# Down projection of a hybrid encoder layer: weight differences in place on VectorE, four fixed operand buffers, another order at the hand-overs

## The chip, the core and the metric

One core of a Trainium2 chip runs the whole program in one launch. The metric is the device time of one execution in microseconds, as the median of several runs. Engines: TensorE multiplies matrices, VectorE and GpSimd do elementwise work, ScalarE does elementwise functions, SyncE's queue (SP) starts the transfers of this part. A matrix product reads operands from SBUF and sums into PSUM.

## What is computed

One layer of an encoder over 512 tokens of width 1024: a mixer of three head groups, a cross-attention into 256 memory tokens, and a gated MLP of inner width 2816 with a causal convolution of width 3. The change lies in the MLP's down projection, the last step.

```python
def conv_ffn(xn, w_up, conv_w, conv_b, w_down):
    h = xn @ w_up
    a, b = jnp.split(h, 2, axis=-1)
    ...
    return (jax.nn.gelu(c, approximate=False) * b) @ w_down

h = h + conv_ffn(rmsnorm(h, ffn_norm_g[l]), ffn_w_up[l], ...)
```

Here `c` is the convolution of `a` along the tokens plus a bias.

## The kernel before

All matrix products are made in three parts: every operand x is split into a high part (ScalarE copies it to the reduced type that TensorE takes) and a low part (VectorE subtracts the high part from x), and high·high, low·high and high·low are summed in PSUM. `split` (lines 325 and 326) makes the two parts.

The up projection goes through 11 groups, `up_group` (line 1353). Each has four PSUM tiles `pa` and `pb` (two of each, 128 features by 512 tokens). Behind the matmuls of a group comes its gating: VectorE reads PSUM with the token scale (lines 1365 and 1372), ScalarE and VectorE make the convolution, ScalarE the GELU, VectorE the product (lines 1375 and 1378). The gated result of group g is two feature blocks of 128, "even" and "odd", over 512 tokens.

The down projection (512 x 2816 times 2816 x 1024) is made with seven block products in place of eight, a Strassen-Winograd scheme. The tokens are halved, the 1024 columns are halved, and each pair of feature blocks (k = 0 to 10) gives the inner halves. So block k has token operands a11, a12, a21, a22 and weights W11, W12, W21, W22 of 128 x 512 each. `operands` (line 1274) makes the token sums. The weight differences are t1 = W12 - W11, t2 = W22 - t1, t3 = W22 - W12, t4 = W21 - t2. The products have numbers: 1 is a11 W11, 6 a sum times t2, 7 a sum times t3, 5 a sum times t1, 2 is a12 W21, 4 is a22 t4, 3 is a sum times W22. A product of one block is six matmuls: two tiles of 128 tokens, three parts each.

The order is a list written out by the code. The first pass, `seq1` (line 1296), takes products 1, 6, 7, 5 for blocks 0 and 1 together, then block by block, then the last two blocks together. The second pass, `seq2` (line 1298), takes products 2, 4, 3, for blocks 0 to 2 together, then singly, then the last two together. Each product sums over all blocks in its own pair of PSUM banks `X[p]`; product 2 goes on summing onto the banks of product 1, product 4 onto those of 7, product 3 onto those of 5, so the second pass continues on sums that VectorE has combined at the end of the first (lines 1427 to 1441: `u2` is products 1 + 6, and so on). The finished quarters of the output are added to the residual `h2T` and stored by `store` (line 1406).

The weights are prepared ahead of their product: `wahead(n)` (line 1341) traces the loads (`wload`, line 1310, on SP's queue) and the preparation (`wprep`, line 1318) three products ahead and at high priority. `wprep` makes t1 and t2 on VectorE (lines 1323, 1324), t3 and t4 on GpSimd (lines 1327, 1330), splits the raw token operands for the second pass (line 1333, 768 columns wide) and splits the weights (line 1338). Raw W11 and W21 lie in a ring of three buffers (`wraw`), the other weights and t2 in a ring of 18 (`r`), of which 16 hold the up projection's token operands until it ends; t1, t3 and t4 lie in a ring of five (`t`). High and low weight parts have rings of five each (`whi`, `wlo`). A scheduler sets the order of the instructions on each engine, by the order of tracing, the priorities and its own timing model; each engine then works its instructions off in that order.

Of the kernel before, what the change touches and what calls it, by code (L numbers as in the profile page):

```python
# [12 lines left out]
AF = mybir.ActivationFunctionType  # L13
# [193 lines left out]
def trunk_body(ctx: ExitStack, tc: tile.TileContext, A):  # L207
# [1061 lines left out]

    op1, op2, raw2 = {}, {}, {}

    def operands(g, even):

# [12 lines left out]
        else:  # L1288
# [6 lines left out]

    seq1 = [(p, k) for ks in ((0, 1), *((k,) for k in range(2, NG - 2)), (NG - 2, NG - 1))
            for p in (1, 6, 7, 5) for k in ks]
    seq2 = [(p, k) for ks in ((0, 1, 2), *((k,) for k in range(3, NG - 2)), (NG - 2, NG - 1))
            for p in (2, 4, 3) for k in ks]
    seq = seq1 + seq2  # L1300
    wd = A["wd"]
    BLK = {"11": 0, "12": 1, "22": 2, "21": 3}
# [15 lines left out]
    def wprep(n):  # L1318
        p, k = seq[n]
        R = lambda b: wr[n >= len(seq1), k, b]  # L1320
        if p == 6:
            wt[1, k], wt[2, k] = ts(), rs()
            V.tensor_tensor(wt[1, k], R("12"), R("11"), ALU.subtract)
            V.tensor_tensor(wt[2, k], R("22"), wt[1, k], ALU.subtract)
        elif p == 7:
            wt[3, k] = ts()
            G.tensor_tensor(wt[3, k], R("22"), R("12"), ALU.subtract)  # L1327
        elif p == 4:
            wt[4, k] = ts()
            G.tensor_tensor(wt[4, k], R("21"), wt[2, k], ALU.subtract)  # L1330
        elif p == 2:
            hi, lo = ma(), ma()
            split(raw2[k], hi[:, 0:3], lo[:, 0:3])
            op2[k] = [(hi[:, i], lo[:, i]) for i in range(3)]
        src = {1: lambda: R("11"), 6: lambda: wt[2, k], 7: lambda: wt[3, k], 5: lambda: wt[1, k],
               2: lambda: R("21"), 4: lambda: wt[4, k], 3: lambda: R("22")}[p]()
        hi, lo = wring("whi", WCFG[2], F32R), wring("wlo", WCFG[3], F32R)
        split(src, hi, lo)
        wx[n] = (hi, lo)
# [13 lines left out]
    def up_group(g):  # L1353
        pa, pb = [ps("a0"), ps("a1")], [ps("b"), ps("b")]
        funit(pa, h2n, range(0, 4), True, False)
        funit(pb, h2n, range(0, 4), True, False)
        funit(pa, h2n, range(4, 8), False, True)
        if g == NG - 1:
            wahead(2)
        funit(pb, h2n, range(4, 8), False, True)  # L1360
        cw = lambda tap, i: pv[:, PC["ffn_conv_w"] + 22 * tap + i:PC["ffn_conv_w"] + 22 * tap + i + 1]
        for c in range(2):
            i = 2 * g + c
            a = ts()
            V.tensor_tensor(a, pa[c], rb2, ALU.mult)
            ca = ts()
            ACT.activation(ca, a, AF.Identity, scale=cw(2, i), bias=pcol("ffn_conv_b", i))
            V.scalar_tensor_tensor(ca[:, 1:S], a[:, 0:S - 1], cw(1, i), ca[:, 1:S], ALU.mult, ALU.add)
            V.scalar_tensor_tensor(ca[:, 2:S], a[:, 0:S - 2], cw(0, i), ca[:, 2:S], ALU.mult, ALU.add)
            ACT.activation(ca, ca, AF.Gelu)  # L1370
            b = ts()
            V.tensor_tensor(b, pb[c], rb2, ALU.mult)
            if c == 0:
                even = b
                V.tensor_tensor(b, b, ca, ALU.mult)
            else:
                raw2[g] = t2("raw2", NG, (P, 3, 256))
                V.tensor_tensor(raw2[g][:, 0:2].rearrange("p a t -> p (a t)"), b, ca, ALU.mult)  # L1378
        operands(g, even)
        if g < 8:  # L1380
            t, l = g % 4, g // 4
            pt = pd("hT")
            for k in range(4):
                PE.transpose(pt[:, k * P:(k + 1) * P], h2[4 * l + k][:, t * P:(t + 1) * P], ident)
            h2T[t, l] = dsl()
            ACT.activation(h2T[t, l], pt, AF.Copy)

    for g in range(NG):
        up_group(g)

    X = {1: [ps("pr") for _ in range(2)], 6: [ps("pd") for _ in range(2)],
         7: [ps("a0"), ps("a1")], 5: [ps("b") for _ in range(2)]}
# [19 lines left out]
    u2 = p5 = None  # L1412
    for n, (p, k) in enumerate(seq):
        wahead(n + 3)
        last = k == NG - 1
        if p == 3 and k >= NG - 2:
            if last:
                for tt in range(2):
                    for m in (n - 1, n):
                        product(m, tt)  # L1420
                    store(0, 1, tt, X[3][tt], h2T[tt, 1])
            continue
        for tt in range(2):
            product(n, tt)
        if not last:
            continue
        if p == 6:
# [4 lines left out]
        elif p == 7:  # L1432
            for tt in range(2):
                V.tensor_tensor(X[7][tt], X[7][tt], u2[:, tt], ALU.add)
        elif p == 5:
            p5 = ma((P, 2, 512), F32)
            for tt in range(2):
                V.tensor_tensor(p5[:, tt], X[5][tt], h2T[2 + tt, 1], ALU.add)
                V.tensor_tensor(X[5][tt], X[5][tt], u2[:, tt], ALU.add)
            for tt in range(2):  # L1440
                store(1, 1, tt, X[7][tt], p5[:, tt])
        elif p == 2:
            for tt in range(2):
                store(0, 0, tt, X[2][tt], h2T[tt, 0])
        elif p == 4:
            for tt in range(2):
                store(1, 0, tt, X[4][tt], h2T[2 + tt, 0])


# [15 lines left out]
```

## Time and profile before

| what | value |
|---|---|
| median of 3 runs | 831.75 us |
| lowest and highest run | 829.24 and 833.24 us |
| the profiled execution's own time | 833.35 us |
| its span in the profile | 831.6 us |
| mean granted TensorE clock of the span | 0.979 |
| TensorE, matmul busy | 799.7 us (96%) |
| VectorE busy | 560.6 us (67%) |
| ScalarE busy | 413.8 us (50%) |
| GpSimd busy | 195.8 us (24%) |

The profile covers one execution. Busy times of an engine say nothing of what waits for what; matmuls overlap in their records, so a busy TensorE is read with the distance from start to start. The granted clock is the share of 2.4 GHz that TensorE was given. Times below are microseconds from the start of the span; the down projection's first matmul begins at 709.78.

### The profile page before, as it was taken

What the parts mean: (1) busy time and instruction counts of PE and PEld (TensorE: products, weight loads), DVE (VectorE), ACT (ScalarE), POOL (GpSimd) and SP (SyncE); (2) the same over time, 40 slices, a digit from 0 to 9 for tenths busy, and PEclk for the clock granted to TensorE, in tenths of its full rate; (3) what the DMA queues carried; (4) which work ended last, traced back from release to release, by engine and by line L of the source; (5) the groups of instructions that cost most, each with busy time, mean ns of one, the idle gap of its engine ahead of it and who ended that gap; (6) DMA issues with size and microseconds to landing.
All of it is one profiled execution on the core that took longest, in us unless ns stands there. A gap on an engine that the chain in (4) does not pass through costs nothing.

```text
span 831.6 us, 11606 instructions
## 1 busy us (share of the span) xinstructions
PE 799.7 (96%) x4130; PEld 659.2 (79%) x4130; DVE 560.6 (67%) x987; ACT 413.8 (50%) x766; POOL 195.8 (24%) x196
## 2 busy tenths in 40 slices
PE   8998997999999998999999999999999999899798
PEld 5775786789897886888888888888888888688586
DVE  6758389356796855745656666666666667997974
ACT  7343453556788854545554444434344334445552
POOL 6556274285741100000100000000000000332440
PEclk9999998999999999999999999999999999999899
DMA  6422022123121334221112322222222223364221
GB/s 206 153 77 75 27 83 96 39 72 108 53 102 38 115 119 135 91 100 51 51 56 97 115 89 101 90 89 101 89 101 90 101 99 105 110 194 142 98 77 76
DMA packets 43625, 79.22 MB, mean 95 GB/s; under 512 B 4784, under 2 KB 5936, under 8 KB 43568
## 3 DMA queue, kind: packets, MB, share of 16 engines
q1 hardware_dynamic: 41328, 75.35, 26.8%
q10 hardware_dynamic: 2240, 3.15, 1.2%
q8 instruction: 32, 0.52, 0.3%
q14 instruction: 25, 0.20, 0.1%
HBM read 76.38 MB, written 2.10 MB: 94 GB/s over the span
## 4 chain that ended last, share of the span: by engine, by line
PE 79%; DVE 6%; ACT 4%; issue 1%; DVEq 0%; ACTq 0%
PE ps L344 19%; PE ps L345 18%; PE ps L346 18%; PE ps L1403 10%; DVE b L658 1%; DVE b L657 1%; PE T L587 1%; DVE wlod L326 1%; DVE ma L326 1%; PE S L344 1%; PE colsum L407 1%; PE tr L535 1%; ACT whid L325 1%; ACT wh L184 1%; PE S L345 1%
## 5 line engine op out<-in xcount | busy, mean ns | idle before, releaser
L184 ACT ACTIVATE wh<-wr 128x512 fp32r<-128x512 f32 x212 | 133.0, 629 | 191.1 <-PE ps L345 130.2
L187 DVE TENSOR_TENSOR wl<-wr,wh 128x512 fp32r<-128x512 f32 x176 | 124.2, 706 | 81.4 <-ACT wh L184 77.1
L344 PE MATMUL ps<-r,wh 128*128 128x512 f32 x416 | 162.2, 393 | 3.1 <-ACT r L325 3.0
L346 PE MATMUL ps<-r,wl 128*128 128x512 f32 x416 | 162.4, 393 | 0.7 <-DVE wl L187 0.7
L345 PE MATMUL ps<-r,wh 128*128 128x512 f32 x416 | 163.0, 392 | 0.0
L344 PEld LDWEIGHTS ps<-r,wh 128*128 128x128 f32 x416 | 78.2, 188 | 20.0 <-ACT r L325 3.7
L1403 PE MATMUL ps<-whid,ma 128*128 128x512 f32 x276 | 89.1, 402 | 4.9 <-ACT whid L325 4.0
L346 PEld LDWEIGHTS ps<-r,wl 128*128 128x128 f32 x416 | 78.7, 189 | 17.8 <-DVE wl L187 1.1
L345 PEld LDWEIGHTS ps<-r,wh 128*128 128x128 f32 x416 | 78.6, 189 | 16.3 <-issue 0.2
L1327 POOL TENSOR_TENSOR t<-r,r 128x512 f32<-128x512 f32 x11 | 18.1, 1646 | 266.5 <-DVE raw L1378 237.8
L344 PE MATMUL ps<-wh,xh 128*128 128x256 f32 (+1 forms) x224 | 72.1, 345 | 8.2 <-DVE d L329 4.7
L345 PE MATMUL ps<-wl,xh 128*128 128x256 f32 (+1 forms) x224 | 77.8, 347 | 0.0
L1403 PEld LDWEIGHTS ps<-whid,ma 128*128 128x128 f32 x276 | 53.6, 195 | 17.1 <-ACT whid L325 4.8
L187 POOL TENSOR_TENSOR wl<-wr,wh 128x512 fp32r<-128x512 f32 x36 | 52.9, 1478 | 31.1 <-ACT wh L184 30.9
L1403 PE MATMUL ps<-wlod,ma 128*128 128x512 f32 x138 | 55.2, 400 | 2.7 <-DVE wlod L326 2.7
L344 PEld LDWEIGHTS ps<-wh,xh 128*128 128x128 f32 x224 | 42.5, 192 | 13.9 <-DVE d L329 4.9
L345 PEld LDWEIGHTS ps<-wl,xh 128*128 128x128 f32 x224 | 43.2, 193 | 5.1 <-issue 0.9
L345 PE MATMUL ps<-xl,wh 128*128 128x512 f32 x112 | 44.7, 402 | 0.0
L346 PE MATMUL ps<-wh,xl 128*128 128x512 f32 x96 | 39.1, 408 | 0.0
L345 PE MATMUL ps<-d,wh 128*128 128x512 f32 x96 | 37.7, 392 | 0.0
L346 PE MATMUL ps<-d,wl 128*128 128x512 f32 x96 | 37.5, 390 | 0.0
L346 PE MATMUL ps<-wh,xh 128*128 128x256 f32 x128 | 37.1, 289 | 0.0
(349 smaller groups left out, 1606.4 us busy)
## 6 DMA issues: line engine op xcount, KB each, us to landing
wr<-in_wp_dram SPq DMA_DIRECT2D x212, 256.0 KB, 2.6
r<-in_wd_dram SPq DMA_DIRECT2D x33, 256.0 KB, 3.5
wrawd<-in_wd_dram SPq DMA_DIRECT2D x22, 256.0 KB, 2.7
r<-in_xt_dram SPq DMA_DIRECT2D x8, 256.0 KB, 5.1
t<-in_xt_dram ACTq DMA_DIRECT2D x8, 256.0 KB, 2.8
out_dram<-t SPq DMA_DIRECT2D x8, 256.0 KB, 2.1
kv<-in_memt_dram ACTq DMA_DIRECT2D x4, 256.0 KB, 4.2
pm<-in_pmat_dram SPq DMA_DIRECT2D x1, 512.0 KB, 4.2
```

What stands on the lines that cost most here:

```text
L184: nc.scalar.activation(hi, raw, AF.Copy)
L187: (nc.vector if el == "V" else nc.gpsimd).tensor_tensor(lo, raw, hi.bitcast(F32), ALU.subtract)
L325: ins = ACT.activation(dhi, src, AF.Copy)
L326: V.tensor_tensor(dlo, src, dhi.bitcast(F32), ALU.subtract)
L344: mm(out, lh, rh, start=start, stop=False)
L345: mm(out, lh, rl, start=False, stop=False)
L346: mm(out, ll, rh, start=False, stop=stop)
L407: mm(pt[:, 2 * i:2 * i + 2], tot[:, i * P:(i + 1) * P], ones[:, 0:2], start=True, stop=True)
L535: PE.transpose(pv4[0:n, c, p, :], src(p, 2 * q + c), ident)
L587: mm(pts[hh].rearrange("p (c h t) -> p c h t", c=2, h=2)[:, c, p], KB[p][o:o + 64, cg, :], RA[p][o:o + 64, cg, :], start=True, stop=True)
L1327: G.tensor_tensor(wt[3, k], R("22"), R("12"), ALU.subtract)
L1403: mm(X[p][tt], l, r, start=not onto and k == 0 and j == 0, stop=k == NG - 1 and j == 2, skip_group_check=onto)
```

## The change

1. In `wprep`, all four differences are made on VectorE and written over their inputs: t1 over W12, t2 over W22, t4 over t2; t3 has a buffer of its own in the ring `r`. GpSimd does nothing more in this stage.
2. The raw token operands of the second pass are split into four fixed pairs of buffers (`ob`), block k into pair k mod 4.
3. `seq2` takes products 2, 3, 4 in place of 2, 4, 3, and the first four blocks together. The last quarter to be stored is now that of product 4.
4. In the last up group the four PSUM tiles are read first (`read`), and the rest of the gating (`rest`) is traced only after six products of the down projection; one more product is prepared ahead of it.
5. At the end of the first pass `p5` is copied by ScalarE, then product 7's sums are added to it; the residual is added and the quarter stored only after product 4 of block 3 is traced.

```diff
@@ seq2
-    seq2 = [(p, k) for ks in ((0, 1, 2), *((k,) for k in range(3, NG - 2)), (NG - 2, NG - 1))
-            for p in (2, 4, 3) for k in ks]
+    seq2 = [(p, k) for ks in ((0, 1, 2, 3), *((k,) for k in range(4, NG - 2)), (NG - 2, NG - 1))
+            for p in (2, 3, 4) for k in ks]
@@ wprep
         if p == 6:
-            wt[1, k], wt[2, k] = ts(), rs()
-            V.tensor_tensor(wt[1, k], R("12"), R("11"), ALU.subtract)
-            V.tensor_tensor(wt[2, k], R("22"), wt[1, k], ALU.subtract)
-        elif p == 7:
-            wt[3, k] = ts()
-            G.tensor_tensor(wt[3, k], R("22"), R("12"), ALU.subtract)
+            wt[3, k], wt[1, k], wt[2, k] = rs(), R("12"), R("22")
+            V.tensor_tensor(wt[3, k], wt[2, k], wt[1, k], ALU.subtract)
+            V.tensor_tensor(wt[1, k], wt[1, k], R("11"), ALU.subtract)
+            V.tensor_tensor(wt[2, k], wt[2, k], wt[1, k], ALU.subtract)
         elif p == 4:
-            wt[4, k] = ts()
-            G.tensor_tensor(wt[4, k], R("21"), wt[2, k], ALU.subtract)
+            V.tensor_tensor(wt[2, k], R("21"), wt[2, k], ALU.subtract)
         elif p == 2:
-            hi, lo = ma(), ma()
+            if k < 4:
+                ob.append((ma(), ma()))
+            hi, lo = ob[k % 4]
             split(raw2[k], hi[:, 0:3], lo[:, 0:3])
@@ up_group
         if g == NG - 1:
-            wahead(2)
+            wahead(3)
...
+        if g == NG - 1:
+            for src, dst in ((pa, av), (pb, bv)):
+                for c in range(2):
+                    read(src, dst, c)
+            return rest
+        rest()
@@ the loop over the products
         wahead(n + 3)
+        if n == 6:
+            rest()
...
+        if p == 4 and k == 3:
+            for tt in range(2):
+                store(1, 1, tt, p5[:, tt], h2T[2 + tt, 1])
...
         elif p == 5:
             p5 = ma((P, 2, 512), F32)
             for tt in range(2):
-                V.tensor_tensor(p5[:, tt], X[5][tt], h2T[2 + tt, 1], ALU.add)
+                ACT.activation(p5[:, tt], X[5][tt], AF.Copy)
                 V.tensor_tensor(X[5][tt], X[5][tt], u2[:, tt], ALU.add)
             for tt in range(2):
-                store(1, 1, tt, X[7][tt], p5[:, tt])
+                V.tensor_tensor(p5[:, tt], X[7][tt], p5[:, tt], ALU.add)
```

**VectorE between the projections, before.** The piece from the last PSUM read of the last up group (`ps_940`) to the low weight part of product 6 of block 1 (`wlod_979`).

```order
L1372 TENSOR_TENSOR t_960_6916<-ps_940_6762,rb_161_892 128x512
L1369 SCALAR_TENSOR_TENSOR t_959_6911<-t_958_6909,pv_78,t_959_6911 128x510
L1323 TENSOR_TENSOR t_976_6945<-r_945_6855,wrawd_942_6849 128x512
L1378 TENSOR_TENSOR raw2_961_6918<-t_960_6916,t_959_6911 128x512
L1324 TENSOR_TENSOR r_977_6946<-r_946_6857,t_976_6945 128x512
L1279 TENSOR_TENSOR sm_962_6920<-t_957_6906,raw2_961_6918 128x256
L1281 TENSOR_TENSOR sm_962_6920<-sm_962_6920,t_957_6906 128x256
L326 TENSOR_TENSOR wlod_979_6950<-r_977_6946,whid_978_6949 128x512
```

The low part stands behind the last PSUM read and most of the last group's gating.

**VectorE between the projections, now.** The low part of product 6 of block 1 is `wlod_957`, its source `r_946`; the last PSUM read is again that of `ps_940`.

```order
L326 TENSOR_TENSOR wlod_953_6872<-r_944_6853,whid_952_6871 128x512
L1365 TENSOR_TENSOR t_960_6913<-ps_939_6761,rb_161_892 128x512
L1323 TENSOR_TENSOR r_985_6991<-r_971_6933,r_970_6931 128x512
L1323 TENSOR_TENSOR r_1005_7069<-r_982_6979,r_981_6977 128x512
L1324 TENSOR_TENSOR r_970_6931<-r_970_6931,wrawd_954_6875 128x512
L326 TENSOR_TENSOR wlod_957_6882<-r_946_6857,whid_956_6881 128x512
L1324 TENSOR_TENSOR r_981_6977<-r_981_6977,wrawd_978_6965 128x512
L1365 TENSOR_TENSOR t_961_6915<-ps_940_6762,rb_161_892 128x512
L1325 TENSOR_TENSOR r_971_6933<-r_971_6933,r_970_6931 128x512
L326 TENSOR_TENSOR wlod_973_6936<-r_951_6867,whid_972_6935 128x512
```

The low part now stands ahead of the last PSUM read, and differences of blocks 2 and 3 stand around it; the gating follows, spread between later rows.

**VectorE between the passes, before.** From the combination of product 7's sums (`ps_971`, `ps_972`) to the third operand split of the second pass's later blocks (`ma_1179`); the low part of product 4 of block 0 comes four rows behind the piece.

```order
L1434 TENSOR_TENSOR ps_971_6939<-ps_971_6939,ma_1116_7465 128x512
L326 TENSOR_TENSOR wlod_1127_7503<-wrawd_1106_7427,whid_1126_7502 128x512
L1434 TENSOR_TENSOR ps_972_6940<-ps_972_6940,ma_1116_7465 128x512
L326 TENSOR_TENSOR wlod_1132_7519<-wrawd_1110_7441,whid_1131_7518 128x512
L1438 TENSOR_TENSOR ma_1133_7528<-ps_973_6941,d_890_6206 128x512
L1439 TENSOR_TENSOR ps_973_6941<-ps_973_6941,ma_1116_7465 128x512
L1438 TENSOR_TENSOR ma_1133_7528<-ps_974_6942,d_906_6393 128x512
L1439 TENSOR_TENSOR ps_974_6942<-ps_974_6942,ma_1116_7465 128x512
L326 TENSOR_TENSOR ma_1157_7616<-raw2_837_5627,ma_1156_7615 128x768
L326 TENSOR_TENSOR ma_1168_7656<-raw2_853_5814,ma_1167_7655 128x768
L1409 TENSOR_TENSOR t_1134_7533<-ps_971_6939,ma_1133_7528 128x512
L326 TENSOR_TENSOR ma_1179_7696<-raw2_869_6001,ma_1178_7695 128x768
```

Splits for blocks 3 and later stand between the additions and ahead of product 4's weights.

**VectorE between the passes, now.** The last 12 of the 24 rows from the operand split of block 0 (`ma_1101`) to the low part of product 3 of block 1 (`wlod_1122`); `ps_968`, `ps_969` are product 5's sums, `ps_966`, `ps_967` product 7's.

```order
L1327 TENSOR_TENSOR r_982_6979<-wrawd_1092_7433,r_982_6979 128x512
L1459 TENSOR_TENSOR ps_968_6923<-ps_968_6923,ma_1095_7445 128x512
L1461 TENSOR_TENSOR ma_1114_7512<-ps_966_6921,ma_1114_7512 128x512
L326 TENSOR_TENSOR ma_1116_7520<-raw2_837_5627,ma_1115_7519 128x768
L326 TENSOR_TENSOR wlod_1118_7524<-wrawd_1092_7433,whid_1117_7523 128x512
L1327 TENSOR_TENSOR r_1002_7057<-wrawd_1125_7563,r_1002_7057 128x512
L326 TENSOR_TENSOR wlod_1120_7534<-r_1096_7450,whid_1119_7533 128x512
L1459 TENSOR_TENSOR ps_969_6924<-ps_969_6924,ma_1095_7445 128x512
L1461 TENSOR_TENSOR ma_1114_7512<-ps_967_6922,ma_1114_7512 128x512
L1424 TENSOR_TENSOR t_1147_7662<-ma_1114_7512,d_890_6206 128x512
L1327 TENSOR_TENSOR r_1014_7107<-wrawd_1133_7599,r_1014_7107 128x512
L326 TENSOR_TENSOR wlod_1122_7544<-r_1099_7462,whid_1121_7543 128x512
```

Only the split of block 3 is left in this piece; splits of later blocks have moved behind it, and differences of product 4 (line 1327) stand in it.

**VectorE in the second pass, now.** The last three differences of product 4 (`L1327`, of blocks 8, 9 and 10), each with its block 21 as `wrawd`; the buffer of `wrawd_1167` is free after `wlod_1158`, that of `wrawd_1170` after `wlod_1166`.

```order
L326 TENSOR_TENSOR wlod_1158_7708<-wrawd_1141_7637,whid_1157_7707 128x512
L1327 TENSOR_TENSOR r_1050_7257<-wrawd_1159_7717,r_1050_7257 128x512
L326 TENSOR_TENSOR ma_1101_7465<-raw2_917_6562,ma_1100_7464 128x768
L326 TENSOR_TENSOR wlod_1161_7720<-r_1144_7649,whid_1160_7719 128x512
L326 TENSOR_TENSOR wlod_1164_7733<-r_1026_7157,whid_1163_7732 128x512
L1327 TENSOR_TENSOR r_1065_7319<-wrawd_1167_7754,r_1065_7319 128x512
L326 TENSOR_TENSOR wlod_1166_7745<-wrawd_1151_7680,whid_1165_7744 128x512
L326 TENSOR_TENSOR ma_1106_7483<-raw2_931_6742,ma_1105_7482 128x768
L326 TENSOR_TENSOR wlod_1169_7757<-r_1154_7692,whid_1168_7756 128x512
L326 TENSOR_TENSOR wlod_1172_7770<-r_1038_7207,whid_1171_7769 128x512
L1327 TENSOR_TENSOR r_1070_7337<-wrawd_1170_7766,r_1070_7337 128x512
```

Before, these differences stood on GpSimd, whose queue held nothing else here; now low parts of other products stand behind them.

## Rows read from the trace of the kernel before

**Rows 1.** Windows of 10 us: length, busy us (instructions) by engine, clock, DMA share, GB/s.
```profile
core 0: us, PE busy (x) PEld busy (x) DVE busy (x) ACT busy (x) POOL busy (x), PEclk, DMA share, GB/s
...
710.00:720.00 10.00, 7.36 (x26) 5.41 (x25) 9.90 (x16) 4.90 (x9) 3.70 (x3) 0.87 0.53 179
720.00:730.00 10.00, 10.00 (x43) 8.17 (x43) 10.00 (x12) 3.87 (x7) 4.31 (x3) 0.96 0.37 110
...
770.00:780.00 10.00, 8.71 (x39) 6.88 (x37) 10.00 (x14) 6.69 (x11) 2.41 (x2) 1.00 0.26 81
780.00:790.00 10.00, 6.43 (x16) 4.47 (x17) 9.53 (x14) 3.21 (x7) 5.83 (x1) 0.66 0.29 105
```

**Rows 2.** Waits of TensorE from 700 to the end: us in total, times, longest.
```profile
PE ps L1403 <- ACT whid L325: 4.0, 2, 3.3
PE ps L1403 <- DVE wlod L326: 2.7, 2, 2.0
PE ps L1403 <- DVE t L1409: 0.9, 1, 0.9
```

**Rows 3.** Groups of instructions by form, 660 to the end: the down projection's matmuls.
```profile
L1403 PE MATMUL ps<-whid,ma 128*128 128x512 f32 x276 | 89.1, 402 | 4.9 <-ACT whid L325 4.0 <-DVE t L1409 0.9
L1403 PE MATMUL ps<-wlod,ma 128*128 128x512 f32 x138 | 55.2, 400 | 2.7 <-DVE wlod L326 2.7
...
L1403 PE MATMUL ps<-whid,d 128*128 128x512 f32 x32 | 10.0, 389 | 0.0
...
L1403 PE MATMUL ps<-wlod,d 128*128 128x512 f32 x16 | 6.2, 389 | 0.0
```

**Rows 4.** Timeline of TensorE: start, length, instruction, count, idle time before it.
```profile
709.78 0.39 PE L1403 MATMUL ps<-whid,ma 128*128 128x512 f32 x1
...
714.70 0.73 PE L1403 MATMUL ps<-whid,ma 128*128 128x512 f32 x2 [0.67 <-ACT whid L325]
717.40 0.76 PE L1403 MATMUL ps<-wlod,ma 128*128 128x512 f32 x1 [1.97 <-DVE wlod L326]
...
758.60 0.39 PE L1403 MATMUL ps<-wlod,ma 128*128 128x512 f32 x1
...
759.96 0.39 PE L1403 MATMUL ps<-wlod,ma 128*128 128x512 f32 x1
...
778.32 0.39 PE L1403 MATMUL ps<-whid,ma 128*128 128x512 f32 x1
781.99 0.48 PE L1403 MATMUL ps<-whid,ma 128*128 128x512 f32 x1 [3.29 <-ACT whid L325]
783.37 1.65 PE L1403 MATMUL ps<-whid,ma 128*128 128x512 f32 x3 [0.89 <-DVE t L1409]
...
827.12 0.39 PE L1403 MATMUL ps<-whid,ma 128*128 128x512 f32 x1
```

**Rows 5.** The chain that ended last: start, length, its longest piece of the second pass.
```profile
785.70 41.36 PE ps L1403 x174
```

**Rows 6.** Timelines of GpSimd (first row) and VectorE (the others).
```profile
719.30 1.66 POOL L1327 TENSOR_TENSOR t<-r,r 128x512 f32<-128x512 f32 x1 [2.84 <-DVE wlod L326]
...
719.75 1.76 DVE L326 TENSOR_TENSOR wlod<-t,whid 128x512 fp32r<-128x512 f32 x1
721.44 0.68 DVE L1324 TENSOR_TENSOR r<-r,t 128x512 f32<-128x512 f32 x1
722.04 1.28 DVE L326 TENSOR_TENSOR wlod<-t,whid 128x512 fp32r<-128x512 f32 x2
```

**Rows 7.** Timelines of ScalarE and VectorE: cast and low part of an operand, 768 wide.
```profile
766.54 0.84 ACT L325 ACTIVATE ma<-raw 128x768 fp32r<-128x768 f32 x1
...
781.77 0.94 DVE L326 TENSOR_TENSOR ma<-raw,ma 128x768 fp32r<-128x768 f32 x1
```

**Rows 8.** GpSimd's wait for block 21; landings of W11 and W21; loads of 694 to 735.
```profile
POOL t L1330 <- DMA wrawd<-in_wd_dram: 10.8, 4, 4.8
...
DMA to landing us min/median/max: 2.4/2.7/5.2
...
r<-in_wd_dram SPq DMA_DIRECT2D x14, 256.0 KB, 4.1
```

More of the change, by code (lines that the diff above doesn't have):

```diff
@@ L1262, in ma @@
         return t2("ma", 18, shape, dt)
-    op1, op2, raw2 = {}, {}, {}
+    op1, op2, raw2, ob = {}, {}, {}, []
     def operands(g, even):
@@ L1335, in wprep @@
         src = {1: lambda: R("11"), 6: lambda: wt[2, k], 7: lambda: wt[3, k], 5: lambda: wt[1, k],
-               2: lambda: R("21"), 4: lambda: wt[4, k], 3: lambda: R("22")}[p]()
+               2: lambda: R("21"), 4: lambda: wt[2, k], 3: lambda: R("22")}[p]()
         hi, lo = wring("whi", WCFG[2], F32R), wring("wlo", WCFG[3], F32R)
@@ L1358, in up_group, with read, gated @@
         if g == NG - 1:
-            wahead(2)
+            wahead(3)
         funit(pb, h2n, range(4, 8), False, True)
         cw = lambda tap, i: pv[:, PC["ffn_conv_w"] + 22 * tap + i:PC["ffn_conv_w"] + 22 * tap + i + 1]
-        for c in range(2):
+        av, bv = {}, {}
+        def read(src, dst, c):
+            dst[c] = ts()
+            V.tensor_tensor(dst[c], src[c], rb2, ALU.mult)
+        def gated(c):
             i = 2 * g + c
-            a = ts()
-            V.tensor_tensor(a, pa[c], rb2, ALU.mult)
-            ca = ts()
+            a, ca = av[c], ts()
             ACT.activation(ca, a, AF.Identity, scale=cw(2, i), bias=pcol("ffn_conv_b", i))
@@ L1370, in up_group, with rest @@
             ACT.activation(ca, ca, AF.Gelu)
-            b = ts()
-            V.tensor_tensor(b, pb[c], rb2, ALU.mult)
+            if c not in bv:
+                read(pb, bv, c)
             if c == 0:
-                even = b
-                V.tensor_tensor(b, b, ca, ALU.mult)
+                V.tensor_tensor(bv[c], bv[c], ca, ALU.mult)
             else:
                 raw2[g] = t2("raw2", NG, (P, 3, 256))
-                V.tensor_tensor(raw2[g][:, 0:2].rearrange("p a t -> p (a t)"), b, ca, ALU.mult)
-        operands(g, even)
+                V.tensor_tensor(raw2[g][:, 0:2].rearrange("p a t -> p (a t)"), bv[c], ca, ALU.mult)
+        def rest():
+            for c in range(2):
+                if c not in av:
+                    read(pa, av, c)
+                gated(c)
+            operands(g, bv[0])
+        if g == NG - 1:
+            for src, dst in ((pa, av), (pb, bv)):
+                for c in range(2):
+                    read(src, dst, c)
+            return rest
+        rest()
         if g < 8:
@@ L1388, in trunk_body @@
     for g in range(NG):
-        up_group(g)
+        rest = up_group(g)
     X = {1: [ps("pr") for _ in range(2)], 6: [ps("pd") for _ in range(2)],
@@ L1414, in trunk_body @@
         wahead(n + 3)
+        if n == 6:
+            rest()
         last = k == NG - 1
-        if p == 3 and k >= NG - 2:
+        if p == 4 and k >= NG - 2:
             if last:
@@ L1420, in trunk_body @@
                         product(m, tt)
-                    store(0, 1, tt, X[3][tt], h2T[tt, 1])
+                    store(1, 0, tt, X[4][tt], h2T[2 + tt, 0])
             continue
@@ L1444, in trunk_body @@
                 store(0, 0, tt, X[2][tt], h2T[tt, 0])
-        elif p == 4:
+        elif p == 3:
             for tt in range(2):
-                store(1, 0, tt, X[4][tt], h2T[2 + tt, 0])
+                store(0, 1, tt, X[3][tt], h2T[tt, 1])
 def kernel(**inputs):
```

## Prediction

> **What bounds the kernel now.** I read the windows of ten microseconds first. Everywhere but in two places of the down projection TensorE is busy all the time; in 710 to 720 it has 7.36 of 10 us, in 770 to 780 8.71, in 780 to 790 6.43, and the granted clock means 0.87 in the first and 0.66 in the last (1.00 is 2.4 GHz, 0.50 is 1.2) [rows 1]. In the same windows VectorE is at 9.53 to 10.00: around both gaps it is the engine that is full. TensorE's own waits in the stage say the same: 4.0 us on ScalarE's high parts, 2.7 us on VectorE's low parts, 0.9 us on VectorE's stores, 7.6 us in all [rows 2].
>
> Now the whole loss. The stage has 276 + 138 + 32 + 16 = 462 matmuls [rows 3]. At full speed six of them, one product of a 128-row weight block, take from 758.60 to 759.96, so 1.36 us or 0.227 us each [rows 4]. 462 x 0.227 is 104.7 us. The first begins at 709.78, the last at 827.12, with its own 0.23 that is 117.6 us. So **12.8 us are lost**: 7.6 of waits, and 5.2 of matmuls that ran at the lower clock after the waits. By place: the last matmul ahead of the second gap begins at 778.32, and behind it come 1 + 3 + 174 = 178 [rows 4, 5]. They should take 178 x 0.2267 = 40.4 us and take 827.12 - 778.32 = 48.8, a loss of 8.4; the first boundary, from the up projection into the down projection, has the other 4.4.
>
> Why VectorE is full: a low part of 128x512 takes 0.68 us alone, and the next begins 0.60 later; the one that begins at 719.75, while a weight difference runs on GpSimd, takes 1.76 and ends 0.55 after GpSimd's 1.66 do [rows 6]. So each of GpSimd's 22 differences (11 of product 7, 11 of product 4) can cost VectorE up to 1.1 us.
>
> **The change, part by part.** *Differences on VectorE.* 22 differences at 0.60 us are 13.2 us more for it; up to 22 x 1.1 = 24 us of stretched instructions go. Per weight block of the first pass it had four low parts and two differences and one stretch, 6 x 0.60 + 1.1 = 4.7 us, and gets seven instructions, 4.2 us, against TensorE's four products, 4 x 1.36 = 5.4. In the second pass it has three low parts, the difference and the 768-wide operand split (0.94 long, so 0.86 to the next [rows 7]), 4 x 0.60 + 0.86 = 3.3 us against 4.1. Both stay under TensorE, so in the steady parts, where TensorE waits for nothing today, this is worth nothing; the gain is at the boundaries.
>
> The Trainium skill's "Perfetto Trace Analysis", section "Optimizing Scalar/DVE Operations", says that work of a saturated VectorE may be moved to ScalarE or even GpSimd, and adds that moves between VectorE and GpSimd might not help, since they share a read port. By its first half alone this change goes the wrong way: see the second rival. The 1.76 us row agrees with its second half.
>
> *First boundary, 4.4 us.* Before, the second block's product 6 stood behind the last group's gating on VectorE, and TensorE waited 0.67 and 1.97 us for it [rows 4]. Now the order has the last group's four PSUM reads and the weights of the first products ahead of the gating: everything for product 6 of block 1 stands before the fourth read. That read can't start before the up projection's last matmul ends, at about 709.95; the product is due three products after 709.78, at 713.9. The lead is near 4 us. Its weights are loaded once the up projection's last matmuls free their buffers; loads into such buffers take 4.1 us here [rows 8], also within that lead. The gating that follows, 13 instructions of VectorE of at most 0.66 us, about 6.5 us in all, is spread over the first six or so blocks, each of which leaves 5.4 - 4.2 = 1.2 us, together with the lead enough. I take the wait as gone: **4.4 us**. From above it could not be more, from below nothing (if the loads come late).
>
> *Second boundary, 8.4 us.* Before, product 4 wrote next onto the PSUM that product 7's sums leave, and its low part stood behind eight additions on PSUM and five operand splits of VectorE. Now four blocks of product 2, and then product 3, come between. From the operand split of block 0 to the low part of product 3's second block VectorE has 24 instructions, 4 of them 768 wide: 20 x 0.60 + 4 x 0.86 = 15.4 us. They start after two ScalarE instructions that follow the end of product 1, the longer of 0.84 [rows 7], say 1.7 us. TensorE has 70 matmuls from there to that low part, 70 x 0.227 = 15.9. So VectorE is late by 1.7 + 15.4 - 15.9 = **1.2 us**, where 8.4 were lost. Whether such a wait drops the clock the rows leave open: after 0.67 us it stayed at full, after 1.97 more it fell [rows 4]. The two drops cost 5.2 us, 2.6 each; I take 0, nearer to 0.67 in kind, and keep 2.6 for the range. ScalarE's two copies take the place of two VectorE additions and hide beside product 2.
>
> *Late differences.* In the second pass a block 21 now is read by VectorE twice and its buffer, one of three, is loaded again only after product 2's low part. In the order the last four differences stand 2.9, 2.7, 2.7 and 2.1 us of VectorE work behind that release, and a load takes 2.7 us to land (2.4 to 5.2) [rows 8] and some 0.2 to be issued. At 2.7 that is 1.2 us of waiting in four rounds that leave 0.8 each: nothing. At 5.2 it is 11.2 - 3.3 = 7.9 us. I take 0.5, as most land near 2.7.
>
> *Fixed operand buffers.* They make block k's split wait for product 4 of block k-4, which ends at least three products, 4.1 us, ahead of the split's use; ScalarE's cast and VectorE's part take 0.84 and 0.94 [rows 7]: 0. The end is as before, two products, two additions and two stores: 0.
>
> **Sum**: 12.8 - 1.2 - 0.5 = 11.1 us. The profiled execution took 833.35 us and goes to 822.2; it lies 1.6 over the median, 831.75, so the forecast is **820.6 us**. Less than 831.75 - 12.8 = 819.0 is only the scatter of the runs, 2.5 us under the median.
>
> **Rivals.** *A stall stays at the second boundary*: another full queue of VectorE takes the old one's place, and its wait drops the clock again. For it: VectorE's 15.4 us there have no slack. Against: TensorE now has 15.9 us of matmuls beside it. Then only the 4.4 come: 827.4.
>
> *VectorE becomes the bound*: if the stretch came from something other than GpSimd and stayed, 13.2 us would fall on an engine that is full for most of the stage, and -11.1 + 13.2 gives 833.9, no change. Against it: the long instruction ends with GpSimd's [rows 6]. By the quoted rule's first half this would be the outcome.
>
> *Slower, blocks that land late*: GpSimd waited 10.8 us in four waits for block 21 [rows 8], and nobody stood behind it; now such a wait stands ahead of low parts on VectorE. Seven differences (of blocks 0 to 2 with 2.4, 1.2 and 1.8 us of cover, and the four above) depend on it. If all land in 5.2 us they wait 22.0 us, of which the rounds' slack takes 5.7: 831.75 - 12.8 + 1.2 + 16.3 = 836.5. It turns the sign at landings of 4.5 us on average; the median of 2.7 speaks against it.
>
> **How the numbers follow.** About 0.5%, 4.2 us, is what a measurement of this kernel can tell from no change. Forecast 0.75, a stall at the second boundary 0.13, VectorE the bound 0.06, late blocks 0.04, 0.02 for the rest. The first is faster, as is most of the second, whose 827.4 lies just past the bound of 827.6: faster 0.86. No change takes the rest of the second and the third: 0.10. Slower 0.04. The range goes from the 819.0 less most of the scatter, 816.8, to 827.0, which takes in the 2.6 of a clock drop, half of the late landings, and nearly all of the first rival.
>
> **What would show it.** Right: no GpSimd row in the stage; low parts of 0.68 us throughout; granted clock 1.00 in 710 to 730; TensorE's waits in the stage under 2 us and the down projection's matmuls within 107 us. Wrong: a wait on a low part of over 2 us behind product 2 with a lower clock behind it (first rival), low parts of over 1 us with no GpSimd beside them (second), differences that begin with a wait for a block 21 load (third).

## The result and the profile after

The changed kernel takes **820.77 us** (median of 4 runs, 816.8 to 821.6), beside 832.5 us for the kernel before (4 runs on the same chip). The ratio is 0.985, 95% interval 0.981 to 0.990. The forecast was 820.6. In the experiments one execution, the profiled one of *first-pass buffers*, took 2149.35 us where the nine others of that kernel took 829 to 835, so it enters no time, and its profile is read for the order of instructions alone.

The windows that answer to [rows 1], same columns:

```profile
710.00:720.00 10.00, 10.00 (x45) 8.27 (x45) 10.00 (x17) 6.63 (x11) 0.00 (x0) 1.00 0.57 185
720.00:730.00 10.00, 10.00 (x46) 8.26 (x45) 10.00 (x18) 5.01 (x10) 0.00 (x0) 1.00 0.36 105
770.00:780.00 10.00, 9.36 (x42) 7.26 (x41) 10.00 (x18) 6.17 (x11) 0.00 (x0) 1.00 0.45 148
780.00:790.00 10.00, 10.00 (x46) 8.27 (x45) 9.80 (x15) 7.53 (x13) 0.00 (x0) 1.00 0.33 116
```

TensorE is full in three of the four, the clock is 1.00 in all, and GpSimd is empty. VectorE is as full as before, and TensorE hardly waits for it any more. All waits of TensorE from 700 to the end (against [rows 2]):

```profile
PE ps L1418 <- DVE wlod L326: 0.6, 1, 0.6
```

TensorE's timeline, the first and last matmul of the down projection and that one wait (against [rows 4]):

```profile
709.82 0.39 PE L1418 MATMUL ps<-whid,ma 128*128 128x512 f32 x1
...
778.24 0.50 PE L1418 MATMUL ps<-wlod,ma 128*128 128x512 f32 x1 [0.64 <-DVE wlod L326]
...
815.36 0.39 PE L1418 MATMUL ps<-whid,ma 128*128 128x512 f32 x1
```

815.36 - 709.82 + 0.23 = 105.8 us, where 117.6 stood. These 11.8 us are the whole difference of the two spans, 831.6 and 819.8. In the chain of waits the last long piece, 174 matmuls before [rows 5], now begins with that wait:

```profile
778.24 37.07 PE ps L1418 x162
```

VectorE's groups from 700 to the end (count | busy us, mean ns), first before and then after, show the stretch that is gone:

```profile
L326 DVE TENSOR_TENSOR wlod<-t,whid 128x512 fp32r<-128x512 f32 x33 | 26.5, 818 | 4.7 <-ACT whid L325 4.7
L326 DVE TENSOR_TENSOR wlod<-wrawd,whid 128x512 fp32r<-128x512 f32 x22 | 19.1, 872 | 4.7 <-ACT whid L325 4.7
L326 DVE TENSOR_TENSOR wlod<-r,whid 128x512 fp32r<-128x512 f32 x22 | 16.6, 761 | 4.1 <-ACT whid L325 4.1
L326 DVE TENSOR_TENSOR ma<-raw,ma 128x768 fp32r<-128x768 f32 x11 | 13.0, 1193 | 0.9 <-ACT ma L325 0.9
```

```profile
L326 DVE TENSOR_TENSOR wlod<-r,whid 128x512 fp32r<-128x512 f32 x55 | 37.1, 690 | 4.9 <-ACT whid L325 4.6
L326 DVE TENSOR_TENSOR wlod<-wrawd,whid 128x512 fp32r<-128x512 f32 x22 | 15.2, 690 | 3.0 <-ACT whid L325 3.0
L326 DVE TENSOR_TENSOR ma<-raw,ma 128x768 fp32r<-128x768 f32 x11 | 10.5, 955 | 1.3 <-ACT ma L325 1.3
```

The same 88 instructions took 75.2 us and now take 62.8. So GpSimd's 22 differences had cost VectorE 12.4 us on the splits. On its other rows some 4 us come to this (the differences t1 of the stage took 858 ns in the mean and now take 690; two rows of the gating are shown under *Engine alone*). That is some 16 us in all, a little more than VectorE now pays to make the differences (22 x 0.60 = 13.2). **By VectorE's time alone the move is nearly a wash.** That opens the question of the experiments: which part of the change gave the 11.8 us?

### The profile page after: what moved, and what is told of

Read it like the earlier page. It is cut to its first block, busy times and chain, and to the rows that moved or that the text cites. A ratio compares the mean times of both kernels' runs of the same rounds, so it can differ in the third digit from the quotient of the medians.

```text
span 819.8 us, 11578 instructions
## 1 busy us (share of the span) xinstructions
PE 793.4 (97%) x4130; PEld 654.6 (80%) x4130; DVE 556.8 (68%) x1009; ACT 414.9 (51%) x768; POOL 156.1 (19%) x174
## 4 chain that ended last, share of the span: by engine, by line
PE 82%; DVE 5%; ACT 2%; issue 1%; DVEq 0%; ACTq 0%
PE ps L344 19%; PE ps L345 19%; PE ps L346 19%; PE ps L1418 11%; DVE b L658 1%; DVE b L657 1%; PE T L587 1%; PE S L344 1%; DVE wlod L326 1%; PE colsum L407 1%; PE S L345 1%; PE S L346 1%; PE tr L535 1%; PE pT L787 1%; PE Sx L344 0%
## 5 line engine op out<-in xcount | busy, mean ns | idle before, releaser
L1418 PE MATMUL ps<-whid,ma 128*128 128x512 f32 x276 | 85.2, 389 | 0.0
L1418 PEld LDWEIGHTS ps<-whid,ma 128*128 128x128 f32 x276 | 51.8, 188 | 10.8
L325 ACT ACTIVATE whid<-r 128x512 fp32r<-128x512 f32 x55 | 34.4, 630 | 29.9 <-PE ps L1418 19.8
L1365 DVE TENSOR_TENSOR t<-ps,rb 128x512 f32<-128x512 f32 x44 | 29.4, 687 | 27.6 <-PE ps L346 27.2
L326 DVE TENSOR_TENSOR wlod<-r,whid 128x512 fp32r<-128x512 f32 x55 | 37.1, 690 | 4.9 <-ACT whid L325 4.6
```

The costliest lines, as they stand in the source:

```text
L325: ins = ACT.activation(dhi, src, AF.Copy)
L326: V.tensor_tensor(dlo, src, dhi.bitcast(F32), ALU.subtract)
L1365: V.tensor_tensor(dst[c], src[c], rb2, ALU.mult)
L1418: mm(X[p][tt], l, r, start=not onto and k == 0 and j == 0, stop=k == NG - 1 and j == 2, skip_group_check=onto)
```

## Experiments

The time of one execution scatters by up to some 4 us to either side of its median. Much of that comes from ahead of the change: the down projection began between 706.47 and 712.34 in the profiles, though no kernel edits that part. So each kernel is read by its **stage**, from the first to the last matmul of the down projection plus 0.23 us, which two profiles of the changed kernel give as 105.8 and 105.7. Each stage is of one profile. The floor is the prediction's 104.7; the one profile in which TensorE has no recorded wait gave 105.4. Each ratio is to the kernel before as run beside that experiment, whose median was 832.5 to 833.8.

| kernel | stage, us | median, us | ratio to before, 95% interval |
|---|---|---|---|
| before | 117.6 | 832.5 | 1 |
| engine alone | 117.3 | 833.82 | 1.001 (0.999 to 1.003) |
| late buffer | 116.9 | 832.15 | 0.999 (0.996 to 1.002) |
| first-pass buffers | none | 834.02 | 1.000 (0.998 to 1.003) |
| order alone | 112.3 | 827.13 | 0.993 (0.990 to 0.995) |
| buffers alone | 110.9 | 827.55 | 0.994 (0.992 to 0.997) |
| in place alone (buffers and engine) | 110.2 | 827.5 | 0.993 (0.990 to 0.996) |
| changed, old product order | 109.9 | 823.85 | 0.989 (0.986 to 0.992) |
| changed, differences on GpSimd | 105.4 | 823.25 | 0.988 (0.986 to 0.991) |
| changed, gating not deferred | 105.8 | 821.23 | 0.986 (0.983 to 0.989) |
| changed, operands from the ring | 106.9 | 821.3 | 0.987 (0.983 to 0.991) |
| changed, again | 105.7 | 821.99 | 0.987 (0.983 to 0.990) |
| changed, GpSimd beside | 112.5 | 828.12 | 0.994 (0.991 to 0.996) |

### One part of the change undone

**Differences of products 7 and 4 back on GpSimd**, with no new buffer:

```diff
-            wt[3, k], wt[1, k], wt[2, k] = rs(), R("12"), R("22")
-            V.tensor_tensor(wt[3, k], wt[2, k], wt[1, k], ALU.subtract)
-            V.tensor_tensor(wt[1, k], wt[1, k], R("11"), ALU.subtract)
+            wt[1, k], wt[3, k], wt[2, k] = rs(), R("12"), R("22")
+            V.tensor_tensor(wt[1, k], R("12"), R("11"), ALU.subtract)
             V.tensor_tensor(wt[2, k], wt[2, k], wt[1, k], ALU.subtract)
+        elif p == 7:
+            G.tensor_tensor(wt[3, k], wt[2, k], R("11"), ALU.subtract)
         elif p == 4:
-            V.tensor_tensor(wt[2, k], R("21"), wt[2, k], ALU.subtract)
+            G.tensor_tensor(wt[2, k], R("21"), wt[2, k], ALU.subtract)
```

> The changed kernel with the two differences of products 7 and 4 back on GpSimd (t3 made as t2 - W11, which is the same difference, over W12; t4 over t2), all else as changed. Stage means the first to the last matmul of the down projection plus 0.23 us; it is 105.8 us in the changed kernel and 117.6 before. Both theories expect stretched VectorE rows (over 1 us) beside GpSimd. Theory A, the prediction's (GpSimd's differences fill VectorE, and that makes the stalls at the boundaries): of the 24 VectorE rows between the passes three differences go (3 x 0.60 = 1.8 us less) and three stretches come (3 x 1.1 = 3.3 us more), so the one wait of 0.64 us grows to about 2.1 and the clock drops behind it (2.6): stage 109 to 110 us, time about 825. Theory B (the order alone gives VectorE its cover, who makes the differences is then of no account): stage under 107 us, time 820 to 822.5.

The stage is 105.4 us, in theory B's range, and not even the 0.64 us wait is left. (Theory B's reason, "the order alone", does not hold: this kernel keeps the new buffers too, and the order alone gives 112.3 below.) Its windows at the second boundary have GpSimd at work and the stretch back on VectorE, and TensorE full:

```profile
770.00:780.00 10.00, 10.00 (x46) 8.28 (x45) 10.00 (x17) 6.00 (x11) 5.90 (x3) 1.00 0.56 181
780.00:790.00 10.00, 10.00 (x46) 8.29 (x45) 9.91 (x13) 7.59 (x12) 6.51 (x3) 1.00 0.48 135
```

```profile
L326 DVE TENSOR_TENSOR wlod<-r,whid 128x512 fp32r<-128x512 f32 x55 | 46.8, 876 | 3.7 <-ACT whid L325 3.6
```

With the rest of the change in place it doesn't matter which engine makes the differences. The median, 823.25 us, lies a little above theory B's 822.5, but this kernel's down projection began at 711.99 in its profile, 2.2 us later than the changed kernel's.

**The last gating traced at once**, in the old order of reads, two products ahead:

```diff
-            wahead(3)
+            wahead(2)
...
-        if g == NG - 1:
-            for src, dst in ((pa, av), (pb, bv)):
-                for c in range(2):
-                    read(src, dst, c)
-            return rest
         rest()
...
-        if n == 6:
-            rest()
```

> The changed kernel with the last group's gating traced at once, reads in the old order, and two products ahead as before; differences, products' order and hand-over as changed. Theory A: the first boundary's 4.4 us come back: a wait for a low part of over 1.5 us near 714 to 718 with a lower clock behind it, stage about 110 us, time about 825. Theory C: the weights run ahead without it; under 1 us comes back, stage 105.8 to 107, time 820.5 to 822.

Stage 105.8 us, and one wait in it, at the second boundary as in the changed kernel:

```profile
PE ps L1413 <- DVE wlod L326: 0.7, 1, 0.7
```

Theory C: with the rest of the change in place the deferral is worth nothing. The deferral alone, in the kernel before, was not run, so whether it would have been enough by itself is open.

**The old product order and hand-over** in the changed kernel:

```diff
-    seq2 = [(p, k) for ks in ((0, 1, 2, 3), *((k,) for k in range(4, NG - 2)), (NG - 2, NG - 1))
-            for p in (2, 3, 4) for k in ks]
+    seq2 = [(p, k) for ks in ((0, 1, 2), *((k,) for k in range(3, NG - 2)), (NG - 2, NG - 1))
+            for p in (2, 4, 3) for k in ks]
```

and the branches of the product loop as before.

> The changed kernel with the second pass and the hand-over between the passes as before (products 2, 4, 3; three blocks first; the copy and the store of the quarter as before). Theory A (the second boundary's loss is the order): of the 8.4 us before all but the stretches come back, so a wait of over 2 us for product 4's weights behind product 2, clock 0.5 to 0.7 behind it, stage 111 to 113 us, time 826 to 828. Rival (the stall before was GpSimd's stretches and its late difference for product 4, in whatever order): stage under 108 us, time under 823.

Stage 109.9 us, between the two: the order is worth 4.2 us here, not 5 to 7, and not under 2. The first boundary stays clean. At the second, TensorE waits at the start of product 4, yet not for that product's weights, as was expected, but for the store's addition that still reads the PSUM on which product 4 is to sum:

```profile
777.10 0.50 PE L1418 MATMUL ps<-whid,ma 128*128 128x512 f32 x1 [2.77 <-DVE t L1424]
```

**The second pass's token operands from the ring of 18** (`hi, lo = ma(), ma()` for each block):

```diff
-            if k < 4:
-                ob.append((ma(), ma()))
-            hi, lo = ob[k % 4]
+            hi, lo = ma(), ma()
```

> The changed kernel with the raw token operands of the second pass split into the next two buffers of the ring of 18, as before, in place of four fixed pairs. Theory A, the prediction's: worth nothing either way, stage 105.3 to 106.3 us, time 820 to 822.5. Rival (the fixed pairs keep splits of later blocks from running ahead of the second boundary's work on VectorE): the splits come earlier in VectorE's order, waits on low parts behind 775 of over 1.5 us, stage 107 to 110 us, time 822.5 to 826.

Stage 106.9 us, between the two ranges: two more waits, 0.30 and 0.21 us, near 783. The rival's mechanism is there, smaller than it said: VectorE's fifth operand split begins 68.3 us into the stage (776.31 - 708.03), 5.7 earlier than in the changed kernel (783.80 - 709.82 = 74.0). The fixed pairs are worth about 1 us of stage, which the times don't resolve.

### One part done alone in the kernel before

**All differences on VectorE and in place** (part 1 of the change, unaltered):

> The kernel before with the first part of the change alone: all four differences on VectorE and in place, order, gating and hand-over as before. Theory A (the loss of 4.4 us at the first boundary sits in the order of the last gating, that of 8.4 at the second in the order of the products; GpSimd's stretches only add a few us): the first boundary keeps over 3 of its 4.4 us, the second loses the two or three stretches in its queue, 2 to 3 us; stage 113 to 116 us, time 828 to 831. Theory C (the first difference waits for a buffer of the ring of five that the last gating holds, and GpSimd's first two differences stretch the gating): in place the weights run ahead of the gating by themselves, the first boundary's 4.4 us go almost whole, and with the stretches of the second the stage is 109 to 112 us, time 823 to 827.

Stage 110.2 us, theory C. No wait is left at the first boundary; the second has the wait that the old product order has above:

```profile
PE ps L1400 <- DVE t L1406: 3.0, 1, 3.0
PE ps L1400 <- DVE ps L1436: 0.2, 1, 0.2
```

Two kernels divide this into buffers and engine. **Buffers alone**: the edit of the first experiment, made to the kernel before, so that the four differences leave the ring of five and two of them stay on GpSimd.

> The kernel before with the differences in the changed places (the first in a buffer of the ring r, the others over their inputs), but those of products 7 and 4 still on GpSimd (t3 made as t2 - W11, the same difference); order, gating and hand-over as before. In-place differences on VectorE alone gave 7.4 us of stage (110.21 against 117.6). Theory E (they gave it by taking GpSimd away, with its stretches): stage 116 to 117.6 us here, time 831 to 833. Theory C (they gave it by leaving the ring of five buffers that the last gating holds, and by having a difference ready earlier): stage 110 to 112 us, time 825 to 828.

**Engine alone**: the same buffers as before.

```diff
-            G.tensor_tensor(wt[3, k], R("22"), R("12"), ALU.subtract)
+            V.tensor_tensor(wt[3, k], R("22"), R("12"), ALU.subtract)
-            G.tensor_tensor(wt[4, k], R("21"), wt[2, k], ALU.subtract)
+            V.tensor_tensor(wt[4, k], R("21"), wt[2, k], ALU.subtract)
```

> The kernel before with the differences of products 7 and 4 made by VectorE in place of GpSimd, in the same buffers of the ring of five; all else as before. Theory E (GpSimd's stretches are the loss): stage 110 to 112 us, time 825 to 828. Theory C (the buffers are): 13.2 us more on VectorE against some 15 us of stretches less is a wash, stage 116 to 118.5 us, time 831 to 834.

Buffers alone 110.9, engine alone 117.3: theory C both times. TensorE's waits with the buffers, then with the engine:

```profile
PE ps L1401 <- DVE t L1407: 3.5, 1, 3.5
PE ps L1401 <- DVE wlod L326: 0.2, 1, 0.2
```

```profile
PE ps L1403 <- ACT whid L325: 5.6, 3, 4.4
PE ps L1403 <- DVE wlod L326: 1.1, 2, 0.7
```

The engine alone makes the first boundary shorter (of the waits of 0.67 and 1.97 us the first is left, and one of 0.39 comes later, at 721.62) and the second longer. Counted to the same matmul behind which the second gap opens, 774.77 - 708.26 = 66.5 us against 778.32 - 709.78 = 68.5 before: 2.0 us gained, and all but 0.3 lost again by a wait of 4.40 us. How the buffers work shows in GpSimd's timeline (a number in brackets is the whole time since the engine's last work, not a loss), first in the kernel before and then with buffers alone:

```profile
713.45 3.01 POOL L1327 TENSOR_TENSOR t<-r,r 128x512 f32<-128x512 f32 x2 [237.82 <-DVE raw L1378]
```

```profile
699.05 1.29 POOL L1326 TENSOR_TENSOR r<-r,wrawd 128x512 f32<-128x512 f32 x1 [223.20 <-issue]
701.75 1.62 POOL L1326 TENSOR_TENSOR r<-r,wrawd 128x512 f32<-128x512 f32 x1 [1.41 <-DVE r L1324]
```

Before, its first difference reads two weights that no gating touches, yet waits for the last product of a gating (L1378): what it waits for is its buffer in the ring of five, which the gating holds. In the ring `r` the same difference is made 14 us earlier, ahead of the boundary.

TensorE's own two waits here were for product 6 of block 1, whose t2 VectorE makes from t1. In the kernel before this t1 lies in the ring of five too. It stands at 711.90, behind the last group's gating up to L1369; with buffers alone it is made at 700.04. Then two rows of the gating, 0.42 us long without GpSimd beside them, are stretched to 1.49 and 1.38 ahead of the low part at 716.67. That stretch is what the engine alone takes away. VectorE before, then with buffers alone:

```profile
711.90 0.69 DVE L1323 TENSOR_TENSOR t<-r,wrawd 128x512 f32<-128x512 f32 x1
...
713.84 1.49 DVE L1279 TENSOR_TENSOR sm<-t,raw 128x256 f32<-128x256 f32 x1
715.37 1.38 DVE L1281 TENSOR_TENSOR sm<-sm,t 128x256 f32<-128x256 f32 x1
716.67 0.68 DVE L326 TENSOR_TENSOR wlod<-r,whid 128x512 fp32r<-128x512 f32 x1
```

```profile
700.04 0.85 DVE L1323 TENSOR_TENSOR r<-r,wrawd 128x512 f32<-128x512 f32 x1 [1.21 <-DMA wrawd<-in_wd_dram]
```

**Only t4 out of the ring of five:**

```diff
-            wt[4, k] = ts()
-            G.tensor_tensor(wt[4, k], R("21"), wt[2, k], ALU.subtract)
+            wt[4, k] = wt[2, k]
+            G.tensor_tensor(wt[2, k], R("21"), wt[2, k], ALU.subtract)
```

> The kernel before with only t4 over t2, still on GpSimd, so that it needs no buffer of the ring of five. In the kernel before the fourth difference of product 4 waits 10.27 us for a buffer that a store of the output holds. Theory C2 (that buffer, or the place that the order finds without it, is 2 to 3 us of the second boundary's 8.4): no GpSimd wait on a store, stage 114.5 to 116 us, time 829 to 831.5. Rival (the second boundary is VectorE's queue alone): stage 117 to 118 us, time 832 to 834.

Stage 116.9 us: neither range, but with 0.7 us gained nearer to the rival. GpSimd no longer waits for a store. The first boundary keeps its 0.67 and 1.97 us, and at the second TensorE's wait for the high part has only become one for the PSUM of product 7:

```profile
PE ps L1403 <- DVE t L1409: 3.5, 1, 3.5
```

**Only the first pass's differences**, as it was meant:

```diff
-            wt[1, k], wt[2, k] = ts(), rs()
+            wt[1, k], wt[2, k] = rs(), R("22")
...
             wt[3, k] = ts()
-            G.tensor_tensor(wt[3, k], R("22"), R("12"), ALU.subtract)
+            G.tensor_tensor(wt[3, k], wt[2, k], R("11"), ALU.subtract)
```

> The kernel before with only the first pass's differences out of the ring of five: t1 in a buffer of the ring r, t2 over W22, t3 over W12 (made by GpSimd as t2 - W11, the same difference); t4 on GpSimd into a buffer of the ring of five as before. The buffers of all four together gave 6.7 us of stage (110.87 against 117.6), with all of the first boundary's loss but a wait of 0.19 us, and a second boundary that still lost some 6. Theory C1 (the first boundary's loss is the wait for buffers that the last gating holds): GpSimd's first difference begins ahead of 706 in place of 713.45, the first boundary loses under 1 us, the second 8.4 as before: stage 113 to 114 us, time 828 to 830. Rival (it takes the late buffer too, or chance in the order): stage 116 to 118 us, time 831 to 834.

As the diff shows, t3 still took a buffer of the ring of five, so only t1 had left it, not t3 as the expectation says. No gain: 1.000 (0.998 to 1.003). There is no stage and no place of the waits. In VectorE's order the low part of product 6 of block 1 now stands ahead of the last PSUM read of the up projection, so t1 did move, and yet the time stayed. Where the loss then sits isn't shown: t3 by itself wasn't tried.

**The product order and hand-over alone**: the third diff of the first part, the other way round, in the kernel before.

> The kernel before with products 2, 3, 4, four blocks first, and the changed copy and store of product 5's quarter; differences (GpSimd, own buffers), gating and operand buffers as before. Theory A (the prediction's sizes, no overlap with the other parts): the second boundary gives back 7.2 of its 8.4 us, the first keeps its 4.4: stage 110.4 us against 117.6 before, time about 825.5. Theory D (the parts overlap; what a part gives depends on the others): putting the old order back into the changed kernel cost 4.2 us of stage (109.94 against 105.77), so if the parts simply add, the order alone gives 4.2: stage 113.4, time about 828.5; more than that only if the in-place differences and the order cure the same stall.

Stage 112.3 us: 5.3 gained, between the sizes of A (7.2) and D (4.2). The first boundary keeps its 0.67 and 1.97 us, at 717.26 and 719.96. The long wait of the second is gone, but two are left, of 0.43 us at 782.80 and, 18 us later, of 1.51. The larger is for the high part of a difference of product 4, for which ScalarE itself waits on GpSimd; TensorE's and ScalarE's timelines:

```profile
800.90 0.73 PE L1403 MATMUL ps<-whid,ma 128*128 128x512 f32 x2 [1.51 <-ACT whid L325]
```

```profile
800.22 0.63 ACT L325 ACTIVATE whid<-t 128x512 fp32r<-128x512 f32 x1 [4.24 <-POOL t L1330]
```

### The disputed cost by itself

**GpSimd beside**: VectorE keeps all its work, and GpSimd makes 22 subtractions that nobody reads.

```diff
+        if p in (7, 4):
+            z = ts()
+            G.tensor_tensor(z, src, src, ALU.subtract)
```

> The changed kernel with 22 more subtractions on GpSimd, one beside each weight split of products 7 and 4, that read the difference which VectorE has made and write a buffer that nobody reads: the result is the same, and VectorE keeps all its own work. It measures what GpSimd costs VectorE here. Theory A (stretches of up to 1.1 us, and VectorE has little room): 4.2 + 1.1 = 5.3 us a block in the first pass against TensorE's 5.4, 3.3 + 1.1 = 4.4 against 4.1 in the second: VectorE becomes the bound at the boundaries and in the second pass, waits on low parts appear, stage 112 to 118 us, time 827 to 833. Rival (the stretches are small or hide): stage under 107 us, time under 822.5.

Stage 112.5 us, in theory A's range: six waits of 0.23 to 1.23 us, all for low parts.

```profile
PE ps L1421 <- DVE wlod L326: 4.1, 6, 1.2
```

The low parts are stretched less than above, and the 88 splits take 69.1 us against 62.8:

```profile
L326 DVE TENSOR_TENSOR wlod<-r,whid 128x512 fp32r<-128x512 f32 x55 | 38.7, 729 | 0.6 <-ACT whid L325 0.6
```

So 22 more subtractions on GpSimd have a price, 6.8 us of stage when nothing is taken off VectorE for them. How much of it is the stretch isn't shown: VectorE's waits for loads also grew, from 1.5 to 6.8 us, and the unread results take buffers of the ring of five, which the last gating and the stores use. That the move between the engines is neutral is read from the engine alone, 117.3 against 117.6.

**The changed kernel again:**

> The changed kernel as it is, once more, for the scatter: the stage should be 105.8 us within 0.4; its start (709.82 in the first profile) shows what the part of the program ahead of it, which no kernel here changes, adds by itself: 709 to 712 in the kernels so far. Time 820 to 823.

Stage 105.7; the start, 706.47, lies below the range that was given, which makes the scatter ahead of the stage larger still.

## Why the prediction was right, and where not

**The total**: 11.1 us were forecast and 11.8 came. The bound was read rightly: 12.8 us were to be had at two boundaries, and the steady parts gave nothing. That the total fits is owed to this bound more than to the account by parts: everything at the two boundaries was won back, but the first step below names another cause than the one that the runs bear out, and the second only half of it. All four signs of being right came true as well, but they can't tell these causes apart.

**First boundary, 4.4 us: right size, but the cause named was not needed.** The step said that the four reads ahead of the gating and the deferral put the weights ahead. Without both, 105.8 us. The new places of the four differences are enough: buffers alone leave a wait of 0.19 us there. The prediction priced GpSimd's wait for block 21 [rows 8], but not that the ring of five keeps t3, and by its place in the order t1, behind the gating. Which of the four buffers does it isn't shown, as t1's alone gave nothing.

**Second boundary, 1.2 us late: right place, wait 0.64.** The count of VectorE's 24 rows against 70 matmuls named the very low part that is late. But the step gave the whole gain to the order. There were two obstacles, product 4's weights and product 7's PSUM. The order alone leaves a wait for the first (1.51 us, later in the second pass), the buffers alone one for the second (3.5 us, and the lower clock behind it). The order gave 5.3 us alone and, with the fixed pairs, 4.4 on top of the in-place differences (110.2 to the 105.8 without deferral); those gave 7.4 alone and, with the pairs, 6.5 on top of the order (112.3 to 105.8). So the two parts nearly add up. Which of the buffers shortens the second boundary isn't shown: t4's alone gave 0.7.

**Differences on VectorE: mis-sized.** "Up to 24 us of stretched instructions" measured 12.4 on the splits, some 16 in all. The prediction didn't book the difference as a gain, so the sum didn't suffer, but its reading of a full VectorE as the cause was off: with GpSimd in the new order VectorE is as full, and TensorE waits for nothing. What counts is what stands ahead of the awaited row in VectorE's order.

**Late differences, 0.5 us: nothing.** VectorE waited three times for block 21, and TensorE never behind it:

```profile
DVE r L1327 <- DMA wrawd<-in_wd_dram: 1.5, 3, 0.8
```

**Fixed operand buffers, 0: about 1 us.** The pairs keep later splits from running ahead.

**Rivals.** A stall did stay, of 0.64 us, and the clock stayed at 1.00. The "2.6 each" for the two drops of the clock, which only the range uses, doesn't follow from the prediction's own figures: 4.4 less 2.64 of waits is 1.8 at the first boundary, and 8.4 less 4.87 is 3.5 at the second. VectorE was not the bound: the stretch ended with GpSimd's work, low parts are 690 ns. The Trainium skill ("Perfetto Trace Analysis", "Optimizing Scalar/DVE Operations") lets a saturated VectorE hand work to GpSimd and warns that this might not help; engine alone, 1.001, agrees with the warning. The skill's "SBUF — State Buffer", section "Who interferes with whom", says that a VectorE instruction with two SBUF inputs contends with a GpSimd instruction that reads SBUF. The groups of low parts agree: 876 ns with GpSimd, 690 without.

## What to carry to other kernels

When an engine waits at a boundary, look in its order and in its helpers' timelines for a wait that its data can't explain: a small ring shared with the previous stage holds a buffer, and moving the result into another ring or over its input may be worth more than moving it to another engine. One buffer of such a ring can be worth nothing alone: t1's and t4's gave 0.0 and 0.7 us, all four 6.7. Two obstacles at one place need two cures: here late weights and a held PSUM bank. The buffers alone, which also cure the first boundary, gave 6.7 us of stage, the order alone 5.3, the whole change 11.8. A sum that comes out right does not show its parts: undo them one by one, and do them one by one. Where runs scatter ahead of the stage, compare the stage's own length.

## What the runs showed of the hardware

In the down projection waits of TensorE of up to 1.51 us left the clock at full speed: 1.00 in 800 to 810 with the order alone, and 1.00 in every window from 710 to 820 with *GpSimd beside* and its six waits of up to 1.23. Those of 1.97 us (each 2.7 us behind one of 0.67) and of 2.77 to 4.40 were followed by a lower one: 0.83 in 720 to 730 with the order alone, behind 1.97, and 0.83 in 780 to 790 with in place alone, behind 3.03. The order alone, then in place alone:

```profile
720.00:730.00 10.00, 10.00 (x37) 8.12 (x38) 8.15 (x14) 4.41 (x8) 7.75 (x2) 0.83 0.54 176
800.00:810.00 10.00, 9.10 (x40) 7.55 (x41) 9.12 (x9) 5.57 (x10) 7.13 (x6) 1.00 0.31 79
```

```profile
780.00:790.00 10.00, 10.00 (x39) 7.92 (x38) 10.00 (x15) 4.93 (x8) 0.00 (x0) 0.83 0.40 131
```
